# Roots spread by transpositions, and raw tiles of a Strassen-like product loaded one step further ahead, in a two-layer decoder trunk

## The chip, the cores and the metric

The kernel runs on one core of one Trainium2 chip. The metric is device microseconds (us) of one execution, of which the median over runs is taken. Beside the timed runs there is one execution that the hardware profiler recorded. Its span goes from the first to the last instruction.

## The reference

The input is x, 1024 positions of 1024 channels, and a conditioning vector c. All is float32. Two layers, each with a token mixer and a feed-forward part, and a last norm:

```python
for i in range(DEPTH):                      # DEPTH = 2
    mod = silu(c) @ ada_w[i] + ada_b[i]     # six shifts, scales, gates
    h = modulate(rms_norm(x, norm_mix_g[i]), sh_m, sc_m)
    y = conformer_conv(h, ...) if i == 0 else multiscale_pool(h, ...)
    x = x + (1.0 + g_m) * y
    h = modulate(rms_norm(x, norm_ffn_g[i]), sh_f, sc_f)
    y = (silu(h @ w_gate) * (h @ w_up)) @ w_down      # 1024 -> 2816 -> 1024
    x = x + (1.0 + g_f) * y
return rms_norm(x, final_g)
```

rms_norm multiplies each position by rsqrt(mean of squares + eps), the position's *root*.

## The kernel before, in words

Channels lie on the 128 partitions, positions along the free axis, in two chunks A and B of 512 positions each; a matmul makes a tile of 128 channels x 512 positions in one PSUM bank. Float32 accuracy comes from splitting: each operand is cast by ScalarE (ACT) into a high part, VectorE (DVE) subtracts it for the low part, and `products` (L491) issues three matmuls per tile, high x high, high x low, low x high. In the trace these are the many `128x512` matmuls of TensorE (PE).

**The roots.** `mean_rsqrt` (L537) gets the sums of squares of 512 positions, with the channels still on the partitions. Four matmuls with a column of 1/D (tile `var`, one output column each) put the mean squares of 4 x 128 positions on the partitions; DVE works out the roots in some ten tiny instructions (tile `col`); then each of four matmuls takes one column of roots, broadcast to 128 x 128, as the stationary operand and the identity matrix as the moving one. The result (tile `rstd`, 128 x 512) holds every position's root on all partitions. These operands are plain float32, not split. The trace has two records for each such matmul, so a set of four shows as eight. The flag `"taps_done"` in `st` is set when the convolution's chunk B has been written out, ahead of the first *joint part* of the feed-forward. After that follow six sets of four (two joint parts, two pool mixers, the norm of A's second feed-forward, the final norm of A) and two sets of two (the final norm of B, in halves of 256 positions).

**The joint parts and the second down stage.** The feed-forward's first products are computed for chunks A and B together by a Strassen-like scheme (tiles `a` and `e`). In layer 1 the down product too goes by seven products of sums, each a row of `Seven` (L1493), over q = 0, 1, 2, 5, 3, 4: p2, p1, p5, p6, p7, p4 and p3. A (product, q) pair is a *step*; I number the steps as the code does: p6 is 14 to 19, p7 is 20 to 25, p4 is 26 to 31. A step with q = 5 is half as wide. Each step needs

- a weight tile: `load` of `weights_of` (L1423) issues its DMA (`raw`, L1449, on SyncE's queue; for some products a second DMA on GpSimd's queue, L1437, adds onto it). For p7 (s3) DVE first adds a kept sum `s` to the raw tile (`raw<-raw,s`), then ACT casts it and DVE makes the low part (`w<-raw,w`);
- an operand: `op<-kinds` (L158, SyncE's queue), which ACT and DVE split into `hi` and `lo`. Four buffers hold the `op` tiles, so the operand of step i+4 can only be fetched when `lo` of step i is done. Five slots hold the raw tiles;
- 24 matmuls (two halves of the operand, four banks, three products each), accumulating into four banks `dn`, first the pair 0, 1, then 2, 3. Products p6 and p7 go on in the same banks: at the end of p6 DVE adds the banks onto x (`x<-dn,gains,x`, L126), and the first matmuls of p7 write into the banks that these instructions have yet to read.

`Seven.run` sets how far ahead loads are issued. In step i it asks for all loads up to and not including i + LOADED + 1, with LOADED = 4 (L1520), and for the splits up to i + SPLIT + 1, with SPLIT = 2. After p7 the six sums `s` are turned into p3's weights: a DMA on GpSimd's queue adds onto each as soon as its `raw<-raw,s` has read it (`s<-in_wds_dram`).

**The order.** PE's order is the order of the code. DVE, ACT, SyncE's and GpSimd's queues get theirs from a list scheduler that works with estimated times. Each engine and each queue executes in order: an instruction or a DMA that waits holds back all behind it.

Of the kernel before, what the change touches and what calls it, by code (L numbers as in the profile page):

```python
# [16 lines left out]
P = 128  # L17
# [45 lines left out]
LOADED = 4  # L63
# [68 lines left out]
def trunk(ctx, tc, xT, c, vec, ada, adan, w1f, w1, wdg, w2, wgu, wdn, wds, wpl, out):  # L132
    nc = tc.nc
    ctx.enter_context(tc.manual_schedule(engines={mybir.EngineType.PE}))
    clock = {"PE": 0.0, "V": 0.0, "G": 0.0, "S": 0.0}
# [5 lines left out]
    last_mm = [None]  # L141
# [3 lines left out]
    def matmul(out, lhsT, rhs, start, stop, more=False):  # L145
        n = out.shape[-1]
        clock["PE"] += n / 2400 * (1 if rhs.dtype == F32R else 4) + 0.0025
        last_mm[0] = nc.tensor.matmul(out, lhsT, rhs, start=start, stop=stop, skip_group_check=more).ins.name  # L148

    def order(ins):  # L150

        if behind[0] and last_mm[0] is not None:
            tc.add_manual_dep(ins.ins, last_mm[0], edge, reason="behind the products")
        return ins
# [41 lines left out]
    def nm(s):  # L196
        uid[0] += 1
        return f"{s}_{uid[0]}"
# [25 lines left out]
    def pace(ahead=AHEAD):  # L224

        for t in [t for t in tasks if t.urgent or getattr(t, "free", False)]:
            while step(t, "V"):
                pass
        moved = True
        while moved and tasks:  # L230
            moved = False
            for e in "VG":
                if clock[e] < clock["PE"] + ahead:
                    moved = any(step(t, e) for t in list(tasks)) or moved
# [62 lines left out]
    def bank(name):  # L297
        return ps.tile([P, 512], F32, tag="mm", name=nm(name))

    def spare_bank(name):  # L300

        return ps.tile([P, 512], F32, tag="ca", name=nm(name), bufs=2)
# [11 lines left out]
    def temp(n, name="t", bufs=0):  # L314
        t = tmp.tile([P, TMPW], F32, tag=name if bufs else "t", name=nm(name), bufs=bufs or 4)
        return t[:, :n]
# [39 lines left out]
    ident = cst.tile([P, P], F32, name="ident")  # L356
# [23 lines left out]
    st = {}  # L380
# [115 lines left out]
    def products(out, wt, k, act, first, last, o=0, n=None, more=False):  # L496

        wk = slice(k * P, (k + 1) * P)
        for i, (wp, a) in enumerate(((0, 0), (0, 1), (1, 0))):
            cols = act[a][:, o : o + n] if n else act[a]  # L500
            matmul(out, wt[:, wp, wk], cols, start=first and i == 0, stop=last and i == 2, more=more)


    def rsqrt(v, y, t, q, alone):

        V_.tensor_scalar(y.bitcast(I32), v.bitcast(I32), -0.5, float(0x5F3759DF), op0=MUL, op1=ADD)
        yield
        V_.tensor_tensor(t, v, y, op=MUL)
        yield
        if not alone:  # L510
            V_.tensor_tensor(t, t, y, op=MUL)
            yield
            V_.tensor_scalar(q, t, 1.0, -10.0 / 3.0, op0=MUL, op1=ADD)
            yield
            V_.tensor_tensor(t, t, q, op=MUL)
            yield
        else:
            V_.tensor_tensor(q, t, y, op=MUL)
            yield
            V_.scalar_tensor_tensor(t, q, -10.0 / 3.0, q, op0=ADD, op1=MUL)  # L520
            yield
        V_.scalar_tensor_tensor(y, t, 5.0, y, op0=ADD, op1=MUL)
        yield
        V_.tensor_tensor(t, v, y, op=MUL)
        yield
        V_.scalar_tensor_tensor(t, t, -0.5 * 0.375**3, y, op0=MUL, op1=MUL)
        yield
        V_.scalar_tensor_tensor(y, t, 1.5 * 0.375, y, op0=ADD, op1=MUL)
        yield

    def mean_rsqrt(acc, n, keep=False, when="stats", loose=False, early=False, then=None):

        count = n // P
        parts = acc if isinstance(acc, list) else [acc]  # L537
        yield when
        b = bank("var")
        for i in range(count):  # L540
            for a in parts:
                matmul(b[:, i : i + 1], a[:, i * P : (i + 1) * P], ones[:, 0:1], start=a is parts[0], stop=a is parts[-1])
        v, t = b[:, :count], b[:, 16 : 16 + count]
        cols = tmp.tile([P, 16], F32, tag="col1", name=nm("col"), bufs=1)
        col, q = cols[:, :count], cols[:, 8 : 8 + count]
        for _ in rsqrt(v, col, t, q, "T" not in st or "taps_done" in st):
            if loose:
                yield
        V_.spent += 0.2
        clock["V"] += 0.2  # L550
        done = V_.last.ins.name
        for ins in [] if loose else recent + (beside if early else []) + [lows[id(wt)][0] for wt in st.get("loaded", [])[1:] if id(wt) in lows]:
            tc.add_manual_dep(ins, done, edge, reason="behind the root")
        recent.clear()
        yield then or ("spread" if loose else "root")
        r = spare_bank("rstd") if "taps_done" in st else bank("rstd")
        for i in range(count):
            matmul(r[:, i * P : (i + 1) * P], col[:, i : i + 1].broadcast_to([P, P]), ident, start=True, stop=True)
        r = r[:, :n]
        if not keep:  # L560
            return r
        held = temp(n, "ny", 2)
        S_.copy(held, r)
        return held
# [54 lines left out]
    def rms(ch, keep=False):  # L619
        acc = yield from sum_sq(x[ch.i], ch.n)  # L620
        return (yield from mean_rsqrt(acc, ch.n, keep))
# [19 lines left out]
    def norm(ch, l, ffn, key, keep=False, squares=None):  # L641
        blocks = [block(f"h{ch.i}", "h") for _ in range(KT)]
        h = st[key] = [(b[:, 0], b[:, 1]) for b in blocks]
        st["blocks", ch.i] = blocks
        if squares is not None:
            rstd = yield from mean_rsqrt(squares.acc, ch.n, keep, loose=ch.i and not l)
        else:
            rstd = yield from rms(ch, keep)
        quiet[0] = ffn and not l
        for k in range(KT):  # L650
            if k == HOLD_TAPS:
                quiet[0] = False
            modulated(ch, l, ffn, h, rstd, k)
            yield
# [4 lines left out]
    def unit(emit, *weights):  # L659
        units.append((weights, emit))  # L660
# [199 lines left out]
    def layer_norm_silu(ch):  # L860
# [30 lines left out]
        if ch.i == 0:  # L891
            for ins in beside:
                tc.add_manual_dep(ins, V_.last.ins.name, edge, reason="behind the sums")
            recent.extend(beside[2:])
            beside.clear()
        rstd = yield from mean_rsqrt(acc, n, when="settled" if ch.i else "stats", early=not ch.i)
        S_.activation(tmp.tile([P, 16], F32, tag="col0", name=nm("col"), bufs=1)[:, 0:1], acc[:, 0:1], AF.Silu)
        hv = [pair(f"h{ch.i}", "v") for _ in range(KT)]
# [109 lines left out]
    def update(ch, d, b, gate, l):  # L1008

        xs = x[ch.i][d]  # L1010
        V_.scalar_tensor_tensor(xs, b, gate[:, l * KT + d : l * KT + d + 1], xs, op0=MUL, op1=ADD)
# [477 lines left out]
    class Seven:  # L1489
# [27 lines left out]
        def run(self, after={}, ending=None):  # L1517
            for i, (name, key, fresh, ends, qs, q) in enumerate(self.steps):
                def emit(take, i=i, name=name, key=key, fresh=fresh, ends=ends, qs=qs, q=q):
                    self.load(i + LOADED + 1)  # L1520
                    if key is None or q != qs[-1]:
                        self.split(i + SPLIT + 1)
                    if key is None:
                        return
                    if fresh and q == qs[0]:
                        self.banks[key] = [spare_bank("dn") if name == "p5" and d > 1 else bank("dn") for d in range(4)]
                    bs, (wt, ops) = self.banks[key], self.ready.pop(i)
                    for ds in ((0, 1), (2, 3)):
                        for j, g in enumerate(ops):
                            for d in ds:  # L1530
                                last = q == qs[-1] and j == len(ops) - 1
                                products(bs[d], wt, 4 * j + d, g, fresh and q == qs[0] and j == 0, last, more=True)
                                if last:
                                    for ch, half in ends:
                                        update(ch, 4 * half + d, bs[d], gate_f, self.l)
                            pace()
                    self.split(i + SPLIT + 1)
                unit(emit)
                if (name, q) in after:
                    after[name, q]()  # L1540
            if ending is not None:
                unit(lambda take: ending([self.ready.pop(i) for i in sorted(self.ready)]))
# [494 lines left out]
```

## Time and profile before

| | |
|---|---|
| median of 3 runs | 1698.97 us (1698.91 to 1699.29) |
| the profiled execution's own time | 1702.04 us |
| its span, first to last instruction | 1700.3 us |
| PE busy | 1670.4 us, 98% |
| DVE busy | 1319.5 us, 78% |
| ACT busy | 800.3 us, 47% |
| GpSimd busy | 481.9 us, 28% |
| mean granted TensorE clock | 0.996 |

The profiled execution is 3.07 us longer than the median, and 1.74 us of it lie outside the span. A row of the timeline view gives the start in us from the span's start, the time from the first start to the last end of the merged instructions, engine, line, operation, tiles and count, and in brackets how long the engine sat idle before it and what released it. Matmuls overlap, so the spacing of their starts counts, not their length.

### The profile page before, as it was taken

The page shows a single profiled execution, that of the slowest core. Times are in us where ns is not written, and L with a number is a line of the kernel's source. Part 1 is how long each engine was busy: PE and PEld are TensorE (multiplying, and loading weights), DVE is VectorE, ACT ScalarE, POOL GpSimd, SP SyncE. Part 2 cuts the span into 40 slices and gives each one's busy share as a digit, 9 for nine tenths or more (in the row PEclk, how much of TensorE's full clock was granted, in tenths as well). Part 3 has the DMA queues.
Part 4 walks back from the last instruction along what each step waited for, and adds up shares of the span by engine and source line. Part 5 has one row for each costly group of instructions (what it writes and reads, how often), then busy time and mean ns, then how long its engine had stood idle before and what let it go on. Part 6 is the DMA issues. An engine that isn't in the chain of part 4 may idle for free.

```text
span 1700.3 us, 21323 instructions
## 1 busy us (share of the span) xinstructions
PE 1670.4 (98%) x7614; PEld 1361.6 (80%) x7614; DVE 1319.5 (78%) x1872; ACT 800.3 (47%) x1085; POOL 481.9 (28%) x566
## 2 busy tenths in 40 slices
PE   7999999999999999999999999999999999999997
PEld 5777777778887888888888888888888888888787
DVE  8889899899758887887666897847877767668576
ACT  3669686867546332333223336646422222234363
POOL 3587767796001111221110211100111111000103
PEclk9999999999999999999999999999999999999998
DMA  8958997828685788886877846877677776586832
GB/s 294 294 173 218 234 237 203 223 76 237 213 241 153 256 258 300 281 263 209 340 271 270 260 160 196 231 242 211 183 225 228 212 231 186 195 280 200 237 137 100
DMA packets 115821, 380.71 MB, mean 224 GB/s; under 512 B 12225, under 2 KB 14401, under 8 KB 115714
## 3 DMA queue, kind: packets, MB, share of 16 engines
q1 hardware_dynamic: 77888, 247.46, 41.2%
q0 software_dynamic: 36736, 130.83, 31.3%
q8 instruction: 60, 0.98, 0.2%
q10 hardware_dynamic: 1090, 1.05, 0.2%
q14 instruction: 47, 0.39, 0.1%
HBM read 311.92 MB, written 63.18 MB: 221 GB/s over the span
## 4 chain that ended last, share of the span: by engine, by line
PE 88%; DVE 5%; DMA 3%; issue 1%; POOL 1%; ACT 1%; SPq 0%; DVEq 0%; ACTq 0%
PE a L148 24%; PE dn L148 23%; PE e L148 13%; PE p L148 12%; PE y L148 6%; PE g L148 3%; PE first L148 3%; PE tap L148 2%; DMA raw<-in_wds_dram 1%; POOL pa L126 1%; PE ada L148 1%; DMA adaw<-in_adan_dram 1%; DVE t L126 1%; PE rstd L148 1%; PE var L148 1%
## 5 line engine op out<-in xcount | busy, mean ns | idle before, releaser
L126 ACT CAST w<-raw 128x1024 fp32r<-128x1024 f32 (+1 forms) x249 | 258.9, 1041 | 367.2 <-PE dn L148 105.8
L148 PE MATMUL dn<-g,w 128*128 128x512 f32 x1152 | 265.1, 390 | 2.4 <-DVE x L126 1.0
L126 DVE TENSOR_TENSOR w<-raw,w 128x1024 fp32r<-128x1024 f32 (+1 forms) x177 | 217.9, 1234 | 50.4 <-ACT w L126 49.9
L148 PEld LDWEIGHTS dn<-g,w 128*128 128x128 f32 x1152 | 215.6, 188 | 48.4 <-DVE x L126 1.4
L148 PE MATMUL a<-n,w 128*128 128x512 f32 x1056 | 247.6, 390 | 1.1 <-DVE n L126 0.7
L148 PE MATMUL p<-h,w 128*128 128x512 f32 x1056 | 244.2, 391 | 0.8 <-DVE h L126 0.6
L126 POOL TENSOR_TENSOR pa<-pa,pr 128x512 f32<-128x512 f32 x160 | 227.8, 1503 | 25.4 <-ACT pr L126 19.2
L148 PEld LDWEIGHTS a<-n,w 128*128 128x128 f32 x1056 | 197.8, 188 | 44.1 <-DVE n L126 2.2
L148 PEld LDWEIGHTS p<-h,w 128*128 128x128 f32 x1056 | 197.2, 188 | 43.9 <-DVE h L126 1.5
L148 PE MATMUL dn<-hi,w 128*128 128x512 f32 (+1 forms) x600 | 174.0, 373 | 1.5 <-DVE x L126 1.5
L126 DVE SCALAR_TENSOR_TENSOR ca<-u,vecs,ca 128x512 f32<-128x512 f32 x245 | 169.9, 748 | 0.5
L126 DVE SCALAR_TENSOR_TENSOR x<-dn,gains,x 128x512 f32<-128x512 f32 (+1 forms) x144 | 100.7, 732 | 39.9 <-PE dn L148 39.8
L148 PEld LDWEIGHTS dn<-hi,w 128*128 128x128 f32 x600 | 109.7, 188 | 22.4 <-ACT hi L126 1.5
L148 PE MATMUL a<-t,w 128*128 128x512 f32 x528 | 123.6, 389 | 0.7 <-DVE w L126 0.7
L148 PE MATMUL e<-b,w 128*128 128x512 f32 x528 | 123.4, 389 | 0.6 <-DVE r L126 0.6
L148 PE MATMUL e<-t,w 128*128 128x512 f32 x528 | 123.2, 389 | 0.0
L126 ACT ACTIVATE pr<-u,vecs 128x512 f32<-128x512 f32 x160 | 108.2, 715 | 25.0 <-POOL pa L126 17.3
L148 PEld LDWEIGHTS a<-t,w 128*128 128x128 f32 x528 | 99.0, 188 | 21.7 <-DVE w L126 1.1
L148 PEld LDWEIGHTS e<-b,w 128*128 128x128 f32 x528 | 99.0, 188 | 21.6 <-DVE r L126 1.0
L148 PEld LDWEIGHTS e<-t,w 128*128 128x128 f32 x528 | 99.1, 188 | 20.6
L1108 POOL DMA_DIRECT2D raw<-in_wgu_dram x41 | 36.2, 884 | 277.8 <-DMA raw<-in_wgu_dram 83.0
L148 PE MATMUL dn<-lo,w 128*128 128x512 f32 (+1 forms) x300 | 111.6, 372 | 0.0
(181 smaller groups left out, 2379.6 us busy)
## 6 DMA issues: line engine op xcount, KB each, us to landing
raw<-in_wgu_dram SPq DMA_DIRECT2D x132, 512.0 KB, 4.8
adaw<-in_ada_dram POOLq DMA_DIRECT2D x48, 512.0 KB, 7.0
raw<-in_wdn_dram SPq DMA_DIRECT2D x44, 512.0 KB, 8.2
raw<-in_wgu_dram POOLq DMA_DIRECT2D x41, 512.0 KB, 7.2
raw<-in_w_dram SPq DMA_DIRECT2D x36, 512.0 KB, 6.2
gd<-g POOLq DMA_DIRECT2D x36, 512.0 KB, 7.8
g<-gd SPq DMA_DIRECT2D x36, 512.0 KB, 5.4
kinds<-k POOLq DMA_DIRECT2D x33, 512.0 KB, 6.9
```

The costliest lines, as they stand in the source:

```text
L126: self.last = self.order(getattr(self.eng, name)(out, *args, **kw))
L148: last_mm[0] = nc.tensor.matmul(out, lhsT, rhs, start=start, stop=stop, skip_group_check=more).ins.name
L1108: d = order(nc.gpsimd.dma_start(w[i], wgu[l, fp, src], accum_op=ADD))
```

## The change

Two edits. `turned` issues TensorE's transpose instead of a matmul with the identity: the same stationary and moving operands, with the transposing mode on. It is used wherever `"taps_done"` is set; the first norms keep the matmul, which now goes through `spread`. The amount by which the planner's clock advances is the same for both. And `Seven.run` asks in step i for the loads up to i + LOADED + 2; `begin`, which loads the first four steps, is unchanged.

```diff
         last_mm[0] = nc.tensor.matmul(out, lhsT, rhs, start=start, stop=stop, skip_group_check=more).ins.name
+
+    def spread(out, columns):
+        matmul(out, columns, ident, start=True, stop=True)
+
+    def turned(out, columns):
+
+        clock["PE"] += P / 600 + 0.0025
+        last_mm[0] = nc.tensor.transpose(out, columns, ident).ins.name
...
         for i in range(count):
-            matmul(r[:, i * P : (i + 1) * P], col[:, i : i + 1].broadcast_to([P, P]), ident, start=True, stop=True)
+            (turned if "taps_done" in st else spread)(r[:, i * P : (i + 1) * P], col[:, i : i + 1].broadcast_to([P, P]))
...
-                    self.load(i + LOADED + 1)
+                    self.load(i + LOADED + 2)
```

PE's order is otherwise unchanged. The scheduler's orders on the other engines move. First, DVE in the mixer stage of chunk A in layer 1, where layer 0's down product of chunk B still runs: `x<-dn` are its updates, which free PSUM banks, `t` belongs to the norm, `win` to the pooling, `adaw` to the conditioning.

```order
 L126 SCALAR_TENSOR_TENSOR t_7991<-x_6042,gains,ny_7958 128x512
 L126 TENSOR_TENSOR win_8028<-hp_7758 128x512
+L126 SCALAR_TENSOR_TENSOR x_7208<-dn_7975,gains,x_7208 128x512
 L126 SCALAR_TENSOR_TENSOR t_7994<-x_6247,gains,ny_7958 128x512
 L126 TENSOR_TENSOR win_8068<-hp_7759 128x514
-L126 SCALAR_TENSOR_TENSOR x_7208<-dn_7975,gains,x_7208 128x512
+L126 SCALAR_TENSOR_TENSOR x_7208<-dn_7976,gains,x_7208 128x512
 L126 SCALAR_TENSOR_TENSOR t_7997<-x_6247,gains,ny_7958 128x512
 L126 SCALAR_TENSOR_TENSOR adaw_7665,mod<-adaw_7665,cact 128x1024
-L126 SCALAR_TENSOR_TENSOR x_7208<-dn_7976,gains,x_7208 128x512
```

Both updates now stand ahead of one `t` more, and the second also ahead of `adaw`.

Second, SyncE's queue where p7's tiles are loaded, before the change. The operands are those of steps 20, 21, 22, 23 and 24, the raw tiles those of steps 20 to 23:

```order
L158 DMA op_12699<-kinds_0_1_206 128x2x512
L158 DMA op_12734<-kinds_1_1_209 128x2x512
L1449 DMA raw_12697<-in_wds_dram 128x1024
L158 DMA op_12757<-kinds_2_1_212 128x2x512
L1449 DMA raw_12732<-in_wds_dram 128x1024
L158 DMA op_12793<-kinds_5_1_221 128x512
L1449 DMA raw_12755<-in_wds_dram 128x1024
L158 DMA op_12833<-kinds_3_1_215 128x2x512
L1449 DMA raw_12791<-in_wds_dram 128x512
```

and after it, the operands and raw tiles of steps 20 to 24:

```order
L166 DMA op_12668<-kinds_0_1_206 128x2x512
L1457 DMA raw_12666<-in_wds_dram 128x1024
L166 DMA op_12703<-kinds_1_1_209 128x2x512
L1457 DMA raw_12701<-in_wds_dram 128x1024
L166 DMA op_12738<-kinds_2_1_212 128x2x512
L1457 DMA raw_12736<-in_wds_dram 128x1024
L166 DMA op_12761<-kinds_5_1_221 128x512
L1457 DMA raw_12759<-in_wds_dram 128x512
L166 DMA op_12797<-kinds_3_1_215 128x2x512
L1457 DMA raw_12795<-in_wds_dram 128x1024
```

Each raw tile now stands right behind the operand of its own step, no longer behind that of the next step.

Third, DVE just ahead of p7's first products, before the change. `raw<-raw,s` are those of steps 22, 23 and 24, `lo` of steps 21 and 22, `w` of steps 21, 22 and 23, and the four `x<-dn` are the updates at the end of p6:

```order
L126 TENSOR_TENSOR raw_12755<-raw_12755,s_12137 128x1024
L126 TENSOR_TENSOR w_12824<-raw_12732,w_12824 128x1024
L126 TENSOR_TENSOR lo_12828<-op_12734,hi_12827 128x1024
L126 TENSOR_TENSOR w_12836<-raw_12755,w_12836 128x1024
L126 TENSOR_TENSOR raw_12791<-raw_12791,s_12164 128x512
L126 TENSOR_TENSOR lo_12840<-op_12757,hi_12839 128x1024
L126 TENSOR_TENSOR w_12872<-raw_12791,w_12872 128x512
L126 SCALAR_TENSOR_TENSOR x_12242<-dn_12214,gains,x_12242 128x512
L126 SCALAR_TENSOR_TENSOR x_12242<-dn_12215,gains,x_12242 128x512
L126 TENSOR_TENSOR raw_12831<-raw_12831,s_12203 128x1024
L126 SCALAR_TENSOR_TENSOR x_12279<-dn_12216,gains,x_12279 128x512
L126 SCALAR_TENSOR_TENSOR x_12279<-dn_12217,gains,x_12279 128x512
```

and after it, from `raw<-raw,s` of step 23 on, with those of steps 24 and 25 behind it, and `lo` of steps 20, 21 and 22:

```order
L126 TENSOR_TENSOR raw_12759<-raw_12759,s_12141 128x512
L126 TENSOR_TENSOR lo_12768<-op_12668,hi_12767 128x1024
L126 TENSOR_TENSOR w_12828<-raw_12701,w_12828 128x1024
L126 TENSOR_TENSOR lo_12832<-op_12703,hi_12831 128x1024
L126 TENSOR_TENSOR w_12840<-raw_12736,w_12840 128x1024
L126 TENSOR_TENSOR raw_12795<-raw_12795,s_12168 128x1024
L126 TENSOR_TENSOR lo_12844<-op_12738,hi_12843 128x1024
L126 TENSOR_TENSOR w_12876<-raw_12759,w_12876 128x512
L126 SCALAR_TENSOR_TENSOR x_12246<-dn_12218,gains,x_12246 128x512
L126 SCALAR_TENSOR_TENSOR x_12246<-dn_12219,gains,x_12246 128x512
L126 TENSOR_TENSOR raw_12835<-raw_12835,s_12207 128x1024
L126 SCALAR_TENSOR_TENSOR x_12284<-dn_12220,gains,x_12284 128x512
```

The first pair of updates now stands behind the raw tile of step 24, and the second behind that of step 25; before, these were steps 23 and 24. Likewise `lo` of step 20 now stands behind the raw tile of step 23, where it stood ahead of that of step 22.

## The prediction

> **What bounds the kernel now.** The page first: busy times, then the chain that ended last.
>
> ```profile
> PE 1670.4 (98%) x7614; PEld 1361.6 (80%) x7614; DVE 1319.5 (78%) x1872; ACT 800.3 (47%) x1085; POOL 481.9 (28%) x566
> PE 88%; DVE 5%; DMA 3%; issue 1%; POOL 1%; ACT 1%; SPq 0%; DVEq 0%; ACTq 0%
> ```
>
> TensorE works almost without a gap, and the chain is 88% PE. So a shorter instruction on PE shortens the end by itself, unless a later instruction was about to wait; a transfer that comes earlier helps only where PE waits. The view of the waits, for PE alone, therefore comes second; here the row of the wait that the change can reach (in us: total, times, longest).
>
> ```profile
> PE dn L148 <- DVE x L126: 2.5, 3, 1.1
> ```
>
> It is small, 2.5 us in all, three waits for updates of x that read the banks PE is about to write. The timeline gives their places below. All sums are in the profiled execution's time (1702.04 us, 3.07 above the median of 1698.97); at the end I subtract the 3.07.
>
> **Transpositions.** PE's timeline around the first set that changes:
>
> ```profile
> 505.88 0.95 PE L148 MATMUL var<-ones,acc 128*128 128x1 f32 x8
> 506.69 5.69 PE L148 MATMUL p<-h,w 128*128 128x512 f32 x24
> 512.22 1.05 PE L148 MATMUL rstd<-ident,col 128*128 128x128 f32 x8
> 513.03 3.23 PE L148 MATMUL p<-h,w 128*128 128x512 f32 x13
> ```
>
> The set holds PE from 512.22 to 513.03, 0.81 us, eight records of 0.101. The `var` set, eight records too, but with one moving column instead of 128, holds it as long (505.88 to 506.69, 0.81). So the price is per record, not per column. That a transpose is one record instead of two is my assumption, as no float32 transpose stands in this trace; with it a set takes 0.40 and saves 0.41. The bounds: nothing saved if it still goes twice, and a loss has no row for it; 0.81 if it were free. I take 0.41, since `var` shows that a record of that kind costs its 0.101 whatever it streams. The other places:
>
> ```profile
> 1673.41 1.05 PE L148 MATMUL rstd<-ident,col 128*128 128x128 f32 x8
> 1687.68 0.60 PE L148 MATMUL rstd<-ident,col 128*128 128x128 f32 x4
> 1688.12 0.28 PE L148 MATMUL var<-ones,acc 128*128 128x1 f32 x2
> 1691.85 1.19 PE L148 MATMUL rstd<-ident,col 128*128 128x128 f32 x4 [1.74 <-DVE col L126]
> 15.76 2.04 PE L148 MATMUL rstd<-ident,col 128*128 128x128 f32 x8 [1.84 <-DVE col L126]
> ```
>
> Six sets of eight lie between 512.22 and 1673.41: 6 x 0.41 = 2.4. The set at 1687.68 takes 0.44 up to 1688.12 and saves 0.22. The last runs after a wait, as the one at 15.76 did, where eight records took 2.04, so about 0.21 each at the spacing of a slow clock; two records fewer save 0.4. Both lie in the tail, where all waits for the roots. Sum: **-3.0 us**, between 0 and, with free sets, -6.2. Around 540 us DVE and not PE leads for a while, but its work there starts from the set at 512.22, so it moves with it.
>
> [...]
>
> **DVE's order in the mixer stage.** The rows of PE and DVE at one of the three waits:
>
> ```profile
> 962.93 1.43 PE L148 MATMUL dn<-g,w 128*128 128x512 f32 x5 [1.03 <-DVE x L126]
> 957.80 0.68 DVE L126 TENSOR_TENSOR win<-hp 128x512 f32<-128x512 f32 x1
> 958.40 0.74 DVE L126 SCALAR_TENSOR_TENSOR t<-x,gains,ny 128x512 f32<-128x512 f32 x1
> 959.67 0.74 DVE L126 SCALAR_TENSOR_TENSOR x<-dn,gains,x 128x512 f32<-128x512 f32 x1
> 962.13 2.06 DVE L126 SCALAR_TENSOR_TENSOR x<-dn,gains,x 128x512 f32<-128x512 f32 x3
> ```
>
> PE resumes at 962.93, when the second update (962.13) is done. In the new order the updates come first and fourth behind the `win` of 957.80: with steps of 0.6 to 0.7 the second starts at about 960.3 and is done at 961.1 instead of 962.9, while PE is ready at 961.9 (962.93 - 1.03). The wait goes: **-1.0 us** (0 if another wait takes its place; no row shows a loss). `adaw`, which is moved back, is waited for by none of PE's rows.
>
> **Five steps instead of four.** The other two waits of that kind, at the passage from p6 to p7:
>
> ```profile
> 1592.46 0.39 PE L148 MATMUL dn<-hi,w 128*128 128x512 f32 x1
> 1593.91 0.47 PE L148 MATMUL dn<-hi,w 128*128 128x512 f32 x1 [1.06 <-DVE x L126]
> 1597.34 0.50 PE L148 MATMUL dn<-hi,w 128*128 128x512 f32 x1 [0.41 <-DVE x L126]
> ```
>
> PE is free at 1592.85 and waits 1.06 and then 0.41. What DVE did:
>
> ```profile
> 1567.37 0.69 DVE L126 TENSOR_TENSOR lo<-op,hi 128x512 fp32r<-128x512 f32 x1
> 1574.15 1.23 DVE L126 TENSOR_TENSOR raw<-raw,s 128x1024 f32<-128x1024 f32 x1 [2.52 <-DMA raw<-in_wds_dram]
> 1586.13 1.23 DVE L126 TENSOR_TENSOR raw<-raw,s 128x1024 f32<-128x1024 f32 x1 [4.77 <-DMA raw<-in_wds_dram]
> 1587.28 1.22 DVE L126 TENSOR_TENSOR w<-raw,w 128x1024 fp32r<-128x1024 f32 x1
> 1590.68 0.69 DVE L126 TENSOR_TENSOR raw<-raw,s 128x512 f32<-128x512 f32 x1
> 1593.02 1.41 DVE L126 SCALAR_TENSOR_TENSOR x<-dn,gains,x 128x512 f32<-128x512 f32 x2
> 1595.39 1.23 DVE L126 TENSOR_TENSOR raw<-raw,s 128x1024 f32<-128x1024 f32 x1 [0.97 <-DMA raw<-in_wds_dram]
> ```
>
> DVE lost 2.52 and 4.77 us to raw tiles that had not landed, and its updates came late by the backlog. If loads were simply earlier, the 1.47 us of PE's waits would go. But the order gives back what it takes: the operands' DMAs cannot move, since operand i+4 waits for `lo` of step i. So a raw tile gains just one place on the queue, and the first updates now stand behind the raw tile of step 24, the second pair behind that of 25. The queues and landings (the landing rows are, in order, the raw tiles issued at 1568.69 and 1590.27, the half-width one of step 23, and those issued at 1593.11 and 1599.14):
>
> ```profile
> 1568.08 0.52 SPq L158 DMA_DIRECT2D op<-kinds  x1
> 1568.69 0.55 SPq L1449 DMA_DIRECT2D raw<-in_wds_dram  x1
> 1593.11 0.59 SPq L1449 DMA_DIRECT2D raw<-in_wds_dram  x1
> 1592.00 2.65 POOL L1437 DMA_DIRECT2D s<-in_wds_dram  x3 [15.12 <-DVE raw L126]
> raw<-in_wds_dram SPq DMA_DIRECT2D x1, 512.0 KB, 5.4
> raw<-in_wds_dram SPq DMA_DIRECT2D x1, 512.0 KB, 5.1
> raw<-in_wds_dram SPq DMA_DIRECT2D x1, 256.0 KB, 6.1
> raw<-in_wds_dram SPq DMA_DIRECT2D x1, 512.0 KB, 10.0
> raw<-in_wds_dram SPq DMA_DIRECT2D x1, 512.0 KB, 13.7
> ```
>
> I follow the new order from 1568.08, where operand 21 is issued once `lo` of step 17 (1567.37) is done, in both kernels. DVE steps take 1.14 (1586.13 to 1587.28), half-width ones 0.6; a raw tile is issued 0.6 behind its operand.
>
> 1. Raw 21 issued at 1568.7, landed after 5.4: 1574.1. DVE: raw 21, `lo` 19: 1576.4.
> 2. Operand 23, raw 23 issued at 1577.0, landed after 6.1: 1583.1. DVE: raw 23, `lo` 20: 1584.8.
> 3. Operand 24, raw 24 issued at 1585.4. The three DMAs that add onto `s` go when raw 23 has been read: they started 1.3 us behind 1590.68, so now at 1584.4, 1.0 ahead of raw 24. In the trace raw 25 stood so (1593.11 against 1592.00) and took 10.0. I take that: 1595.4.
> 4. DVE: raw 24, `lo` 22, `w` 23 (2.9), so the first update starts at 1598.3, done at 1599.0 instead of 1593.7. PE waits 6.2 instead of 1.06.
> 5. Raw 25 is issued at about 1587.7 (behind `lo` 21, 2.3 later) and lands after 10.0 at 1597.7; DVE is done with the first pair at 1599.7 and with raw 25 at 1600.8; the third update ends at 1601.5, and PE needs it at 1601.7 (half a step, 12 products at the spacing of 0.227 that 24 products in 5.5 us have, is 2.7). The 0.41 go.
>
> Sum: 6.2 - 1.47 = **+4.7 us**. The bounds: three landings of 5.1 would end the first update at 1592.8, when PE is free, and the sum is -1.5; with 13.7 for raw 25 the third update ends at 1603.2, 1.5 late, and it is +6.2. That ScalarE's casts come in time, as they did behind 1586, is taken for granted.
>
> A wait of 6 us has a second price.
>
> ```profile
> 12.05 1.86 PE L148 MATMUL var<-ones,acc 128*128 128x1 f32 x8 [6.03 <-DVE acc L126]
> 84.89 5.74 PE L148 MATMUL g<-h,w 128*128 128x512 f32 x24
> 93.17 7.33 PE L148 MATMUL a<-h,w 128*128 128x512 f32 x24
> 93.00:97.00 4.00, 4.00 (x13) 3.17 (x13) 3.66 (x9) 2.81 (x5) 4.00 (x4) 0.57 1.03 320
> ```
>
> After 6.03 idle the `var` set took 1.86 instead of 0.95, and where the granted clock (the 0.57 in the last row) fell once in the stream, 24 products took 7.33 instead of 5.74. So **+1.6 us** (0 if the clock holds, as behind the wait of 1.06); a wait of 6.2 is nearest to the 6.03. [...]
>
> Total: -3.0 - 1.0 + 4.7 + 1.6 = **+2.3 us**.
>
> **The rivals.**
> - *The loads come in time.* Against it: the 10.0. For it: 5.1 and 5.4 in the same stretch. If the three landings (21, 23, 24) sum to no more than 15.3, no wait is left: -3.0 - 1.0 - 1.5 = -5.5, 1693.5 us.
> - *Half in time.* Raw 24 is not held by the three DMAs and takes 6.1: the update ends at 1595.1, PE waits 2.3, no clock loss: -3.0 - 1.0 + 0.8 = -3.2, 1695.8 us.
> [...]
> - *A float32 transpose still goes twice* (the change does not do what it says). For it: each float32 matmul of this trace has two records. Total -1.0 + 4.7 + 1.6 = +5.3, 1704.3 us, slower. It decides once a set saves less than 0.26 of its 0.81: the six and the tail then give less than 1.9, and 4.7 + 1.6 - 1.0 - 1.9 is 3.4 us.
>
> **How the numbers follow.** A difference of 0.2%, 3.4 us, is about what a measurement of this kernel can tell from none. Forecast 0.40: 1698.97 + 2.3 = 1701.3, no change that can be told. Loads in time 0.20, half in time 0.20, four times faster 0.05, twice 0.15. The range takes in the nearer half of the first rival (1693.5 and some waits left) and, above, the forecast with raw 25 at 13.7 (+1.5, 1702.8) and most of the last: 1694.0 to 1704.0. Faster by over 0.2% (below 1695.6): the first rival and a fifth of the second, 0.24. Slower (above 1702.4): the last, and a quarter of the forecast, for raw 25: 0.25. The same: 0.51.
>
> **What would show it.** `rstd` sets with 4 records at 0.10 spacing (8: the last rival; 0.05: a quarter of the price); no wait at 962.9; DVE's `raw<-raw,s` of step 24 waiting about 7 us and PE waiting some 6 at p7's start, at a lower clock behind it. Wrong if raw 24 lands within 6 us, or if PE's waits at p7 vanish.

## The result, and the profile after

| | before | changed |
|---|---|---|
| median of 21 runs | 1698.78 us (1697.17 to 1702.89) | 1700.81 us (1698.56 to 1857.26) |
| ratio, 95% interval | | 1.0013 [1.0007, 1.0019] |
| the profiled execution | 1702.04 us, span 1700.3 | 1701.31 us, span 1699.5 |

The change makes the kernel slower by 0.13%, 2.0 us at the medians, which is less than the 0.2% that I called "the same". The forecast was +2.3. The run of 1857.26 us, at a mean granted clock of 0.851, is left out of the ratio.

The two profiled executions stand the other way round, so the first question is where their spans differ. The same stretch of each, before any instruction that the change touches (TensorE alone; the columns are busy time and count, granted clock, DMA share and GB/s). Before:

```profile
92.00:101.00 9.00, 9.00 (x49) 0.81 1.05 304
```

and after:

```profile
92.00:101.00 9.00, 9.00 (x49) 1.00 1.05 304
```

The clock fell there in the profiled execution of before and not in that of the changed kernel; nine microseconds at 0.81 are 1.7 lost. The change is not what decides this: a second profile of the changed kernel (e9 below) has 0.81 there too. By the first `var` set near 505 the profile of before is already 2.23 behind. So I compare profiles from the start of that set to the end of the span: before 1700.3 - 505.88 = 1194.4, changed 1699.5 - 503.65 = 1195.9.

**The page after.**

```profile
PE 1668.0 (98%) x7586; PEld 1358.5 (80%) x7586; DVE 1319.8 (78%) x1872; ACT 799.2 (47%) x1085; POOL 488.3 (29%) x566
PE 88%; DVE 6%; DMA 2%; issue 1%; POOL 1%; ACT 1%; SPq 0%; DVEq 0%; ACTq 0%
```

28 matmul records less, and 1% more of the chain on VectorE.

**The transposes.** The timeline at the first set that changed:

```profile
503.65 0.95 PE L148 MATMUL var<-ones,acc 128*128 128x1 f32 x8
509.99 0.60 PE L156 MATMUL rstd<-ident,col 128*128 128x128 f32 x4
510.35 10.02 PE L148 MATMUL p<-h,w 128*128 128x512 f32 x43
```

and the groups of tile `rstd` (ns: shortest, median, longest; first and last start):

```profile
L148 PEld LDWEIGHTS rstd<-ident,col x40: 185/190/334, 15.5 to 441.7; 128*128 128x128 f32 x40
L148 PE MATMUL rstd<-ident,col x40: 271/275/551, 15.5 to 441.8; 128*128 128x128 f32 x40
L156 PEld LDWEIGHTS rstd<-ident,col x28: 133/135/138, 509.8 to 1691.7; 128*128 128x128 f32 x28
L156 PE MATMUL rstd<-ident,col x28: 270/272/294, 510.0 to 1691.8; 128*128 128x128 f32 x28
```

Four records in place of eight; the set holds PE for 0.36 us (509.99 to 510.35), 0.09 per record, where 0.81 stood. A set saves 0.45.

**The mixer stage.** One wait is left, 24 products further on, 0.24 in place of 1.03:

```profile
964.48 13.90 PE L148 MATMUL dn<-g,w 128*128 128x512 f32 x60 [0.24 <-DVE x L126]
```

**From p6 to p7.** PE's timeline:

```profile
1587.66 0.39 PE L148 MATMUL dn<-hi,w 128*128 128x512 f32 x1
1591.80 0.77 PE L148 MATMUL dn<-hi,w 128*128 128x512 f32 x1 [3.75 <-DVE x L126]
```

and the granted clock (the number behind the count) of two stretches there:

```profile
1590.00:1595.00 5.00, 3.21 (x8) 0.55 1.02 266
1595.00:1600.00 5.00, 5.00 (x19) 0.77 1.03 286
```

The wait is 3.75 where 1.06 stood, and the clock fell: the first matmul takes 0.77 where it took 0.47. VectorE began the eight updates behind p5 at 1562.10 in before:

```profile
1562.10 5.36 DVE L126 SCALAR_TENSOR_TENSOR x<-dn,gains,x 128x512 f32<-128x512 f32 x8
```

and after (with the two queues; the SyncE rows are the operand of step 21, and the raw tiles of steps 24 and 25):

```profile
1555.33 5.35 DVE L126 SCALAR_TENSOR_TENSOR x<-dn,gains,x 128x512 f32<-128x512 f32 x8
1588.02 1.22 DVE L126 TENSOR_TENSOR raw<-raw,s 128x1024 f32<-128x1024 f32 x1 [7.29 <-DMA raw<-in_wds_dram]
1590.90 1.40 DVE L126 SCALAR_TENSOR_TENSOR x<-dn,gains,x 128x512 f32<-128x512 f32 x2
1592.86 1.23 DVE L126 TENSOR_TENSOR raw<-raw,s 128x1024 f32<-128x1024 f32 x1 [0.55 <-DMA raw<-in_wds_dram]
...
1561.30 0.52 SPq L166 DMA_DIRECT2D op<-kinds  x1
1577.98 0.57 SPq L1457 DMA_DIRECT2D raw<-in_wds_dram  x1
1580.21 0.80 SPq L1457 DMA_DIRECT2D raw<-in_wds_dram  x1
...
1576.83 2.65 POOL L1445 DMA_DIRECT2D s<-in_wds_dram  x3 [11.78 <-ACT w L126]
```

The three adds onto `s` go 1.15 ahead of raw 24, raw 24 takes 10.0 (1577.98 to 1588.02), VectorE waits 7.29 for it, and the updates that PE waits for stand behind. That is the forecast's mechanism, with a shorter wait than the forecast's 6.2.

**The tail.** A new wait, and the last set:

```profile
1682.86 0.61 PE L148 MATMUL var<-ones,acc 128*128 128x1 f32 x4 [0.49 <-DVE acc L126]
1691.70 0.40 PE L156 MATMUL rstd<-ident,col 128*128 128x128 f32 x2 [1.74 <-DVE col L126]
```

**Where the stretch went.** The `var` sets ahead of the fifth and the sixth set, before and after:

```profile
1165.96 0.95 PE L148 MATMUL var<-ones,acc 128*128 128x1 f32 x8
1665.48 0.95 PE L148 MATMUL var<-ones,acc 128*128 128x1 f32 x8
```

```profile
1161.70 0.95 PE L148 MATMUL var<-ones,acc 128*128 128x1 f32 x8
1665.21 0.95 PE L148 MATMUL var<-ones,acc 128*128 128x1 f32 x8
```

Up to the fifth set the changed kernel gains 2.0 (4.26 less the 2.23 from outside). From the fifth to the sixth, where the second down stage lies, it takes 503.51 in place of 499.52 and so loses 4.0. From there to the end it gains 0.5. Sum +1.4.

### The profile page after: what moved, and what is told of

Same layout as the page of the kernel before. It is cut to its first block, busy times and chain, and to the rows that moved or that the text cites. A ratio compares the mean times of both kernels' runs of the same rounds, so it can differ in the third digit from the quotient of the medians.

```text
span 1699.5 us, 21268 instructions
## 1 busy us (share of the span) xinstructions
PE 1668.0 (98%) x7586; PEld 1358.5 (80%) x7586; DVE 1319.8 (78%) x1872; ACT 799.2 (47%) x1085; POOL 488.3 (29%) x566
## 4 chain that ended last, share of the span: by engine, by line
PE 88%; DVE 6%; DMA 2%; issue 1%; POOL 1%; ACT 1%; SPq 0%; DVEq 0%; ACTq 0%
PE a L148 23%; PE dn L148 23%; PE e L148 13%; PE p L148 12%; PE y L148 6%; PE g L148 3%; PE first L148 3%; PE tap L148 2%; POOL pa L126 1%; PE ada L148 1%; DVE t L126 1%; DMA raw<-in_wds_dram 1%; DVE x L126 1%; DMA adaw<-in_adan_dram 1%; PE var L148 1%
```

## The experiments

Theory: the transposes gain, and five steps lose more, because the first updates behind p6 now stand behind raw 24 on VectorE, and raw 24 lands late for the adds onto `s`. Rivals: the gain of the transposes is eaten by later waits; the wait only moves when it is removed; raw 24 is held by something else. The two kernels and the twelve experiments stand in one table. "Stretch" is from the first `var` set to the end of the span, "5 to 6" from the fifth `var` set to the sixth, both from the one profiled execution of each, in us. All ratios are within 0.3% of 1, so "faster" and "slower" below mean only that the interval leaves out 1.

| kernel | median | ratio to before, 95% | stretch | 5 to 6 | waits at p7's start |
|---|---|---|---|---|---|
| before | 1698.78 | | 1194.4 | 499.5 | 1.06, 0.41 |
| changed | 1700.81 | 1.0013 [1.0007, 1.0019] | 1195.9 | 503.5 | 3.75 |
| e1 transposes alone | 1696.15 | 0.9985 [0.9976, 0.9994] | 1190.0 | 497.5 | none |
| e2 five steps alone | 1702.71 | 1.0023 [1.0015, 1.0032] | 1197.6 | 503.3 | 3.15 |
| e3 updates first | 1697.18 | 0.9987 [0.9978, 0.9996] | 1190.5 | 496.8 | none |
| e4 without the adds onto s | 1696.24 | 0.9985 [0.9976, 0.9994] | 1189.6 | 497.1 | none |
| e5 before again | 1698.95 | 1.0003 [0.9994, 1.0012] | 1194.8 | 499.8 | 1.20, 0.41 |
| e6 adds in turn | 1699.71 | 1.0007 [0.9998, 1.0016] | 1195.1 | 501.8 | 3.15 |
| e7 14 matmuls in the wait | 1700.97 | 1.0018 [1.0009, 1.0026] | 1193.6 | 500.7 | 0.42 |
| e8 all sets transposed | 1698.65 | 1.0002 [0.9993, 1.0011] | 1192.2 | 499.7 | 0.30 |
| e9 changed again | 1701.43 | 1.0015 [1.0006, 1.0024] | 1194.3 | 501.0 | 2.91, 0.68 |
| e10 10 matmuls in the wait | 1700.36 | 1.0007 [0.9998, 1.0015] | 1194.6 | 501.2 | 1.33 |
| e11 e1 with the sum ahead | 1697.41 | 0.9988 [0.9979, 0.9997] | 1191.5 | 498.3 | none |
| e12 e3 with the sum ahead | 1696.21 | 0.9985 [0.9976, 0.9994] | 1190.2 | 496.8 | none |

**e1, the transposes alone.**

```diff
-                    self.load(i + LOADED + 2)
+                    self.load(i + LOADED + 1)
```

> The transposes alone, loads four steps ahead. My theory: each of the six sets saves 0.45 us as in the changed kernel's trace, the tail about 0.4, the wait of the mixer stage 0.8; all of it on the path, so -3.5 to -4 and about 1695 us, ratio 0.9977; the p6-to-p7 waits stay at about 1 and 0.4. Rival (the shorter sets are eaten by a wait later on, and five steps cost little): within 1 us of before, ratio 0.9995 to 1.0005.

1696.15, -2.6 us (-4.1 to -1.0): the gain is on the path, a little less than expected. The p7 waits did not stay: VectorE lost 1.44 for raw 22, not the 4.77 of before, and began the first updates at 1585.58; PE did not wait. VectorE:

```profile
1578.33 1.22 DVE L126 TENSOR_TENSOR raw<-raw,s 128x1024 f32<-128x1024 f32 x1 [1.44 <-DMA raw<-in_wds_dram]
1585.58 1.40 DVE L126 SCALAR_TENSOR_TENSOR x<-dn,gains,x 128x512 f32<-128x512 f32 x2
```

**e2, five steps alone.** The reverse: `turned` is taken out, and the matmul with the identity stands in all sets.

> Five steps alone, matmuls with the identity as before. Theory A (the chain of raw tiles hangs on TensorE's progress, so the wait is the same wherever TensorE stands): the wait at the start of p7 is 3.5 to 4 in place of 1.47 and the clock drops behind it, +4 us, 1702.8, ratio 1.0024. Theory B (the chain runs at its own pace): TensorE comes 3 us later to p7 than in the changed kernel, waits about 1, the clock holds, ratio 1.000.

PE at p7's start:

```profile
1595.07 0.76 PE L148 MATMUL dn<-hi,w 128*128 128x512 f32 x1 [3.15 <-DVE x L126]
```

and the stretch behind it, at a clock of 0.50:

```profile
1595.00:1600.00 5.00, 4.93 (x12) 0.50 1.04 302
```

1702.71, +4.0 us (+2.5 to +5.4), as theory A had it; only the wait is a little under A's 3.5 to 4. TensorE came 3.87 us later to the end of p6 than in the changed kernel (1591.92 against 1588.05; 1.65 of this stood already at the first `var` set), yet the wait shrank by only 0.60. From the issue of operand 21 to the end of p6 it is 26.7 us in both profiles, so the chain of raw tiles moves with TensorE's own progress. With e1 this settles the first question: the two edits pull in opposite directions, -2.6 and +4.0, and their sum, +1.4, is within the interval of the change's +2.0 (+1.2 to +3.2).

**e3, the updates first.** The adds of raw 24 and 25 are ordered behind the first and the second pair of updates, as they stood to them before the change. Only VectorE's order moves, by these two rows.

```diff
                 V_.tensor_tensor(r, r, st["sum", q], op=ADD)
+                if q in LAST[1:]:
+                    tc.add_manual_dep(V_.last.ins, st["updated", q - 3], edge, reason="behind the updates")
...
                                         update(ch, 4 * half + d, bs[d], gate_f, self.l)
+                                    st["updated", ds[0] // 2] = V_.last.ins.name
```

> The whole change, with the adds of raw 24 and 25 ordered behind the first and the second pair of x updates on VectorE. My theory (the updates wait only because they stand behind raw 24): no wait at the start of p7, no drop of the clock, 3.1 + 0.8 + 1.5 less than before: about 1693.5 us, ratio 0.997. Rival (the wait moves to the first product that needs the weights or operands queued behind raw 24): a wait of 2 to 4 in steps 21 to 25 and a ratio near 1.000.

VectorE at the passage:

```profile
1587.56 1.40 DVE L126 SCALAR_TENSOR_TENSOR x<-dn,gains,x 128x512 f32<-128x512 f32 x2
1589.63 1.23 DVE L126 TENSOR_TENSOR raw<-raw,s 128x1024 f32<-128x1024 f32 x1 [0.66 <-DMA raw<-in_wds_dram]
```

No wait at p7's start; raw 24 lands about as late as in the changed kernel (9.8 after its issue at 1579.82), and PE does not wait for it. So the late updates were the cause of the wait. The median, 1697.18, misses the 1693.5 that I expected (1698.8 less 5.4). Of the 5.4, transposes and mixer stage were counted as 3.9 and gave 2.6 in e1, and the 1.5 of p7's waits may be missing in a typical run of before; what is left lies within the interval. No run separates the parts.

**e4, without the adds onto `s`.** Six DMAs are left out, so p3's weights lack a term.

```diff
-            if kind in ("s1", "s4"):
-                plus(r, src(3 if kind == "s1" else 1))
+            if kind == "s1":
+                plus(r, src(3))
```

> The whole change without the six DMAs on GpSimd's queue that add onto the sums s, so that p3's weights lack a term; all orders else are the same. My theory (these DMAs make raw 24 land after 10.0): raw 24 lands after 4 to 6, VectorE is through with it 4 to 6 us earlier, the wait at the start of p7 is under 0.5, about 1694 us, ratio 0.997. Rival (raw 24 is held by the operands and raw tiles of SyncE's own queue): still 9 to 10, a wait of 3 to 4, ratio 1.001.

The issue of raw 24, and VectorE's instruction that reads it:

```profile
1580.40 0.55 SPq L1457 DMA_DIRECT2D raw<-in_wds_dram  x1
1586.90 1.23 DVE L126 TENSOR_TENSOR raw<-raw,s 128x1024 f32<-128x1024 f32 x1 [3.74 <-DMA raw<-in_wds_dram]
```

Raw 24 lands after 6.5 in place of 10.0, and the wait at p7 is gone though the order of VectorE is that of the change. The adds are what makes raw 24 late by the last 3.5 us; with SyncE's own queue alone it takes 6.5.

**e5, the kernel before once more** (blank lines alone added).

> The kernel before once more, for a second profile of it. Ratio 1.000. My theory: its 1.06 and 0.41 us of waits at the start of p7 hung on raw 22, which took 9.2 us to land in the first profile and 6.5 in that of the transposes alone, where no wait stood; so here anything from 0 to 1.5, and the first update done up to 1.8 us ahead of its need where the landing is short. Rival: the waits belong to four steps without transposes and stand here as before, 1.3 to 1.6 in all.

VectorE at raw 22, and PE at p7's start:

```profile
1585.13 1.22 DVE L126 TENSOR_TENSOR raw<-raw,s 128x1024 f32<-128x1024 f32 x1 [4.90 <-DMA raw<-in_wds_dram]
1592.91 0.47 PE L148 MATMUL dn<-hi,w 128*128 128x512 f32 x1 [1.20 <-DVE x L126]
```

The rival: the same waits, 1.20 and 0.41, and raw 22 as late as in the first profile. But e8, with the same order and four steps, has 0.30, and e1 and e11 none. Why raw 22 lands after 6.5 in e1 and after 9.4 here stays open. The rows show a candidate that no run tried alone: GpSimd's first add onto `s` starts 0.9 ahead of raw 22's issue in before, here and in e8, where raw 22 lands after 9.2, 9.4 and 8.2; it starts 1.7 ahead in e1, where raw 22 lands after 6.5.

**e6, the adds in turn.** p3's adds are issued in the order in which p7 frees the sums, so that they don't wait for each other and start one at a time. Only one row moves, that of q = 5 by two places on GpSimd's queue.

```diff
-                plus(r, src(3 if kind == "s1" else 1))
+                to = st.setdefault("adds", [4, 3, 5, 2, 1, 0]).pop()
+                plus(st["sum", to], wds[to, 1][:, : duo_width(to) * 512])
```

> The whole change, with p3's six adds onto s issued in the order in which p7 frees the sums (q = 0, 1, 2, 5, 3, 4 in place of 0, 5, 1, 2, 3, 4), so that they go one at a time and not three at once; all else stands in the same order. My theory (raw 24's 10.0 us came of the three at once): raw 24 lands after 5 to 7, the wait at p7's start is under 0.5, the clock holds: 1696 to 1697, ratio 0.9985. Rival (the adds only move ahead and slow raw 21 to 23 instead): the same wait of 2 to 4, ratio 1.001.

VectorE's raw tiles of steps 22, 23 and 24, and PE:

```profile
1575.39 1.23 DVE L126 TENSOR_TENSOR raw<-raw,s 128x1024 f32<-128x1024 f32 x1 [2.31 <-DMA raw<-in_wds_dram]
1579.22 0.69 DVE L126 TENSOR_TENSOR raw<-raw,s 128x512 f32<-128x512 f32 x1 [2.60 <-DMA raw<-in_wds_dram]
1588.24 1.23 DVE L126 TENSOR_TENSOR raw<-raw,s 128x1024 f32<-128x1024 f32 x1 [3.79 <-DMA raw<-in_wds_dram]
...
1592.01 0.49 PE L148 MATMUL dn<-hi,w 128*128 128x512 f32 x1 [3.15 <-DVE x L126]
```

The rival was right. Raw 24 itself takes 6.5 now, but raw 22 and 23 are waited for 2.31 and 2.60 (1.03 and 0.99 in the changed kernel), so raw 24 is issued later and the updates come as late. "Three at once" was the wrong half of my theory: issued one at a time, the adds delay the tiles ahead of raw 24 instead, and e4, which takes them away, is the one of the two that helps. Whether their number or their bytes hold the tiles, no run shows.

**e7 and e10, TensorE kept busy in its wait.** 14, then 10, matmuls into a bank that nobody reads, between p6 and p7.

```diff
+                    if name == "p7" and q == qs[0]:
+                        for _ in range(14):
+                            nc.tensor.matmul(self.banks["y"][0], wt[:, 0, :P], ops[0][0], start=True, stop=True, skip_group_check=True)
```

> The whole change, with 14 more matmuls of 0.23 us between p6 and p7, into a bank that nobody reads, so that TensorE is busy through most of its wait. My theory (some 1.6 us of the loss is the lower clock behind an idle TensorE): p7's first real product starts where it did, at full clock: 1.6 less than the change, about 1699.2, ratio 1.0003. Rival (the slow products have another cause than the idle time): clock 0.5 to 0.8 again and ratio 1.0013 or more.

> The whole change with 10 more matmuls between p6 and p7 (14 in the run before): 2.3 us of work, so that some 1.2 of the wait are left. My theory (the lower clock comes of TensorE's idle time): the clock holds at 1.00 behind p7's start, and from the var set to the end 2 to 2.5 less than the changed kernel, some 1193.5. Rival (that is what the profile of the 14 showed by luck, since its median gained nothing): clock 0.5 to 0.8 behind p7's start, and from the var set to the end 1195 to 1197.

PE in e7:

```profile
1591.94 3.33 PE L1538 MATMUL dn<-hi,w 128*128 128x512 f32 x14
1595.11 0.39 PE L148 MATMUL dn<-hi,w 128*128 128x512 f32 x1
1598.41 0.50 PE L148 MATMUL dn<-hi,w 128*128 128x512 f32 x1 [0.42 <-DVE x L126]
```

and in e10:

```profile
1596.16 0.50 PE L148 MATMUL dn<-hi,w 128*128 128x512 f32 x1 [1.33 <-DVE x L126]
```

The clock stayed at 1.00 in both (1590 to 1600), as theory had it. That the fall behind p7's start comes of the idle TensorE is likely with this, but two profiles don't prove it, as the clock can hold over 2.91 us of idle time too (e9). And the time gained little: e7's median is no better than the changed kernel's, and e10's 1.1 better than that of e9, its neighbour, with intervals that overlap; e10's stretch is 1194.6, not the 1193.5 expected. The rows suggest why: at full clock PE reaches the second pair of updates sooner, and waits 0.42 and 1.33 there, for raw 25. Between the fifth and the sixth set e7 and e10 take 500.7 and 501.2, and so does e9 (501.0), where the clock held without any filling; only the first profile of the change, where it fell, takes 503.5. In e7 the filling also outlasts the wait: VectorE's first update is done at about 1594.3, and p7's first product starts at 1595.11.

**e9, the changed kernel once more.**

> The changed kernel once more, as the neighbour of the next three and for a second profile of it. From the start of the var set ahead of the first transposes to the end of the span it took 1195.85 us, against 1194.42 and 1194.85 in the two profiles of before. My theory (the wait at p7's start hangs on the order of the instructions and comes in every execution): 1195.5 to 1196.5 again, a wait of 3.2 to 3.8 and a lower clock behind it; ratio 1.0013. Rival (the wait was luck of one execution's transfers): under 1 us of wait, 1190 to 1192 from var to the end.

PE at p7's start, both pairs:

```profile
1593.39 0.47 PE L148 MATMUL dn<-hi,w 128*128 128x512 f32 x1 [2.91 <-DVE x L126]
1597.05 0.50 PE L148 MATMUL dn<-hi,w 128*128 128x512 f32 x1 [0.68 <-DVE x L126]
```

with the clock at 1.00:

```profile
1590.00:1595.00 5.00, 2.09 (x10) 1.00 1.05 277
1595.00:1600.00 5.00, 4.32 (x20) 1.00 1.04 298
```

The wait is there again, 2.91, but the clock held, and the second pair was waited for. So the wait belongs to the order, and the clock's fall to some executions only. Wait and stretch (1194.3) both missed my range on the low side.

**e8, transposes in all sets.** `turned` also in the five sets ahead of `"taps_done"`, with four steps.

> Transposes in all norms, the first five sets too, loads four steps ahead. My theory: 0.45 us for each of the five sets more, all on the path: 2.2 under the transposes alone, about 1694, ratio 0.997. Rival (in the first 500 us other waits end last): within 1 us of the transposes alone, ratio 0.998 to 0.999.

The first products of the program:

```profile
19.56 5.74 PE L148 MATMUL first<-h,w 128*128 128x512 f32 x13 [2.98 <-ACT h L126]
```

The rival, and more: 1698.65, no better than before. Of the five sets only the second gives its 0.45: from its start to the third `var` set 118.0 in place of 118.5 (e5). From the third, fourth and fifth `var` set to the next the distances are those of e5 within 0.1, because the products behind these sets wait for their operands (behind the fourth set 0.80 where e5 has 0.34, behind the fifth 0.66 where it has 0.20). And the first set costs: the first products wait 2.98 where 1.65 stood, and 1.64 once more at 29.80, a wait that no other profile has; from the first `var` set to the second it is 82.5 where e5 has 80.3. A last part lies in p7. The wait at its start is small (0.30), but the next product, p4, waits for the updates at p7's end:

```profile
1624.22 0.47 PE L148 MATMUL dn<-hi,w 128*128 128x512 f32 x1 [1.30 <-DVE x L126]
1625.39 0.50 PE L148 MATMUL dn<-hi,w 128*128 128x512 f32 x1 [0.24 <-DVE x L126]
```

**e11 and e12, the sum ahead.** In the tail, VectorE's add of the sum for B's last norm stands ahead of A's three last products, as before the change; e11 on e1, e12 on e3.

```diff
+            while k == 1 and ("added", 0, 1) not in st:
+                yield "wait"
             (V_ if k % 3 == 1 else G_).tensor_tensor(xs, xs, rstd, op=MUL)
+            if k % 3 == 1:
+                tc.add_manual_dep(V_.last.ins, st["added", 0, 1], edge, reason="behind the sums")
```

> Transposes alone, with the sum that B's second half needs put ahead of A's three last products on VectorE again, as it stood before. My theory (that order gave back the 0.45 of the last full set): the 0.49 of wait before the var set near 1677 goes, 0.45 less than the transposes alone: from the first var set to the end 1189.5, median about 1695.7, ratio 0.998. Rival (the tail hangs on other chains, or the three products come late): no gain, 1190.0 from var to the end.

> The whole change with the adds of raw 24 and 25 behind the updates, and the sum ahead as in the run before. Between the var set of the pool mixer of B and that of the last norm of A the pinned kernel took 496.8 us, the transposes alone 497.5, so my theory (five steps are worth those 0.7 once nothing stands behind raw 24): 0.5 to 0.7 less than the run before, 1189.0 from var to the end, median near 1695.3. Rival (five steps are worth nothing even so): the same as the run before within 0.3.

PE in the tail of e11:

```profile
1679.54 0.61 PE L148 MATMUL var<-ones,acc 128*128 128x1 f32 x4 [0.97 <-DVE acc L126]
```

My theory fell: the wait in the tail is 0.97, more than the 0.49, and from the sixth `var` set to the end e11 takes 34.8 and e1 34.3. In the order, a later add now stands behind one update more; whether that is the cause was not tried. So what holds the tail stays open. Between the fifth and the sixth set e12 takes 496.8 again, as e3 did, and e1 and e11 497.5 and 498.3: five steps do make that stage shorter by 0.7 to 1.5 in these profiles, once the updates stand first. Part of this is waits at p7's end: 0.20 in e1, 0.41 and 0.23 in e11, none in e3 and e12. In the medians (1696.21 against 1697.41, intervals that overlap) it is not shown.

**The best version.** e1, e3, e11 and e12 are all faster than both kernels by 0.1 to 0.3%, with intervals that lie below 1 and below the changed kernel's; among the four nothing can be told. e1 is the simplest: keep the transposes, leave the loads at four steps.

## Why the prediction came out

The total was right, 1701.3 against 1700.81. The mechanism was right too, that of the transposes and that of the updates behind raw 24 (e1 to e4). That the total came out within a microsecond was luck, as two errors offset each other: transposes and mixer order were forecast at -4.0 and gave -2.6 (e1; -4.1 to -1.0, so by the medians -4.0 is just possible, and the traces below show the parts that were missing), five steps were forecast at +6.3 (4.7 + 1.6) and gave +4.0 (e2; 2.5 to 5.4).

- *Transposes, -3.0.* The record count and the price of 0.10 were right: 0.09, a set saves 0.45 where 0.41 was forecast. Up to the fifth set the distances between the `var` sets shrink by 0.35 to 0.45 each (where no other wait lies). The trace has 0.36 for 0.81, 2.25 times faster, nearly all of it from the records that are gone (four for eight). No run shows the "four times faster" of the chances: four records at a spacing of 0.05 would take 0.20, and they take 0.36. The wrong part is the tail: from the sixth set on I counted 0.41 + 0.22 + 0.4, and against e5 (34.25 from the sixth `var` set to the end) the changed kernel gains nothing (34.29). A new wait of 0.49 stands there, behind an order of VectorE that I had not looked at; with the order put back (e11) the wait was 0.97, so its cause stays open. And the last set, where I counted 0.4 at the spacing of a slow clock, takes 0.68 in e5, with the matmuls too, and not the 1.19 of the first profile (at a granted clock of 0.50, 1691.5 to 1693.2).
- *Mixer stage, -1.0.* 1.03 and 1.50 in the two profiles of before, and 0.24 or 0.25 in eight profiles with the new order. But it is 0.83 to 0.85 in three others of the new order (e3, e10, e11), and 0.31 in e2, which has the old one. So the order may help, but e2's row shows that the wait is also short without it, and a whole microsecond was too much.
- *The wait, 6.2.* It was 3.75 and 2.91. Steps 2 to 4 held in their sum: raw 24 took 10.0, and from operand 21's issue to the first update passed 29.6 (1561.30 to 1590.90; forecast 30.2). Inside step 2 two errors offset each other: raw 23 landed after 4.0 (1571.54 to 1575.50), not 6.1, but `lo` of step 19 came 1.5 later behind operand 21 than forecast, as it waited 1.67 for ScalarE's cast, which the forecast had taken for granted. What failed is the start of step 1, "I follow the new order from 1568.08 ... in both kernels". Operand 21 was issued 24.8 ahead of p6's end in before (1592.85), but 26.7 in the changed kernel (1588.05) and as much in e2 (1565.18, 1591.92). VectorE was ahead already at the end of p5: its eight updates there began 6.8 us earlier (1555.33 against 1562.10), TensorE stood only 4.8 earlier at p6's end. Those two microseconds are taken off the wait. All of it need not come of the fifth step: with four steps the same lead is 24.5 in e5, but, reckoned from the fifth `var` set, about 26 in e1 and e11.
- *"The 0.41 go".* No: raw 25 took 12.7 (1580.21 to 1592.86), not 10.0. Where the clock held, the second pair was waited for: 0.68, 0.42, 1.33.
- *The clock, +1.6.* It fell in three of the four profiles with the long wait (3.75; 3.15 in e2 and e6; not at 2.91). Behind the 3.75 the next 13 products took 5.59 (1591.80 to 1597.39), where at 0.227 they take 3.0: 2.6 lost. But e7, e9 and e10 show that a part of it (0.4 to 1.3) is waited for raw 25 where the clock holds. The two terms were not independent. Beside e9, where the clock held, the stage of the first profile is 2.5 longer (503.5 against 501.0), so where the clock fell it cost more than 1.6, and where it held nothing; how often it falls in a run without a profile is not known.
- *The rivals.* "Still goes twice" falls with the 28 records and the 0.36. "Loads in time" falls with every profile of the change. "Half in time" had a wait of 2.3 with the clock held, which e9 comes near to (2.91), but raw 24 was held all the same: it landed after 9.7 there.

What stays open: a profile is one execution. Those of before took 3.3 and 1.7 us more than its median, those of the changed kernel 0.5 and nothing, so the profiles' stretches (-0.5 to +1.4 between the two of each) show less of a loss than the medians do (+2.0). If the 1.5 us of p7 waits are absent from most runs of before, as they are from e1 with the same order there, that would be the missing part; no run here shows it.

## What to carry to other kernels

When loads are issued earlier, look at what the waiting engine has queued behind the first tile that comes late: a list scheduler that believes its own transfer times can put a blocked add ahead of work that the bottleneck needs (here the add of raw 24, which waited 7.29 us). Here an edge that puts the urgent work first (e3, 1697.18 us) was worth more than moving the transfers (e6, 1699.71 us), which only moved the delay. And don't add the price of a slow clock to a wait without asking for what comes next: the time that one wait takes, the next may already have been owed (where the clock held, the second pair cost 0.42 to 1.33 us).

## What the runs showed of the hardware

- The stationary load of a float32 transpose takes 135 ns where that of the matmul took 190, and it goes once (28 records, where before has 56); the moving pass keeps its length (272 against 275 ns a record).
- At p7's start the clock held at 1.00 over 2.91 us of idle TensorE (e9) and fell over 3.15 (in e2 to 0.50, in e6 to 0.73, as means over 5 us) and over 3.75 (to 0.55, in the first profile of the change); in e6 the first matmul after the wait still ran at full speed (0.49) and the clock fell behind it. The length of the idle time does not explain the stretch from 92 to 101, where only 0.7 to 1.4 us of it stand among small matmuls: the clock fell there in 6 of the 14 profiles (0.81 in before), behind 0.94 to 1.43 us, and held in the others, behind 0.68 to 1.44. And behind 6.03 us of idle time at the start of before the `var` set took 1.86 in place of 0.95, while the granted clock reads 1.00 there.
- Raw tile 24 of 512 KB landed after 6.5 us with SyncE's queue alone (e4) and after 9.0 to 10.0 in the profiles where three adds went ahead of it on GpSimd's queue (the changed kernel 10.0, e2 9.4, e3 9.8, e7 9.0); with one half-width add 1.1 ahead (e6) it took 6.5 as well.
